# Differential heads: the low part of the keys beside zeros, so that every product of the scores works on 128 rows

## The chip, the cores and the metric

One core of a Trainium2 chip runs the whole program in one launch. The metric is device microseconds of that core, the median of several runs. The engines are named as the profile names them: PE is the tensor engine (PEld its weight loads), DVE the vector engine, ACT the scalar engine, POOL the gpsimd engine, SP the queue that starts the DMAs.

## What is computed

Two transformer blocks over 512 tokens of width 2048, all in float32. The first block has 16 meta tokens ahead (528 in all), eight grouped-query heads with an axial rope, and eight differential heads; the second has stick-breaking attention and a gated linear recurrence. The change is in the differential heads, each of which has two maps of 64 features:

```
q1, q2 = q[:, :, 0], q[:, :, 1]        # 64 features each
k1, k2 = k[:, :, 0], k[:, :, 1]
s1 = einsum('bhqd,bhkd->bhqk', q1, k1) * scale + bias
s2 = einsum('bhqd,bhkd->bhqk', q2, k2) * scale + bias
a  = softmax(s1) - lam * softmax(s2)
o  = einsum('bhqk,bhkd->bhqd', a, v)
```

## The kernel before

Precision comes from splits: a float32 operand becomes a high part, rounded to float32r, and a low part, the rest. A product is then three products: high with high, high with low and low with high. ACT rounds (line 148), DVE subtracts (line 149). The projections do this over 16 tiles of 128 rows (`fm` and `tm`, PSUM tile `pj`); their weights come from `in_wp` half a unit (512 KB) at a time, are split into the tile `wsp` (three buffers) and are consumed in a fixed sequence.

The order of PE is written out at tracing: projections (`main_work`) and all other pieces (`sides`) are generators, and `run` takes the next step of the first of them whose keys are there by a modelled clock. Each PE instruction is chained to the one before, so PE's order is fixed. The other engines take their instructions in the order that a scheduler gives them, each queue first in, first out.

The differential heads' scores are `b_scores` (lines 649 to 700), once per head h. With 64 features per map, the 128 rows of the array hold two things: plane m of the tile `qq` (`q2t`) has the high part of map m's queries in 64 of its rows and the low part in the other 64, and plane m of the tile `kk` (`kb`) has the high part of map m's keys in both halves. One product of 128 rows so gives high with high plus low with high. The third product, high with low, takes the 64 rows of `q2t` that hold the high part, and plane 2 of `kb`, where rows 0 to 63 hold the low part of map 0's keys and rows 64 to 127 that of map 1's.

`scores(qt, m, l)` does this for 128 queries (qt) and one map (m); the 528 keys go in two halves c of 264 columns into the PSUM tile `pss` (one buffer). So one call has four products on PE, two of 128 rows and then two of 64:

```
mm(s[:, c, :HL], q2t[:, m, qsl], kb[:, m, c * HL : (c + 1) * HL], True, False)          # line 674
mm(s[:, c, :HL], q2t[rows, m, qsl], kb[rows, 2, c * HL : (c + 1) * HL], False, True)    # line 676
```

There are 8 heads x 4 query tiles x 2 maps = 64 calls. DVE adds the distance bias and takes the row minimum out of `pss` (line 680), which frees it; ACT takes the exponential (683); DVE joins the two maps (693 to 696) into a tile `e`, which `pv_steps` transposes through `ptt` and `pmt` and multiplies with the values. The copies into `kb` are lines 660 to 663 (ACT) and 664, 665 (DVE); the bias table of a head is line 653 (POOL). Each head asks for a new tile `kk`, of which there is one buffer, so a head's copies wait until the head before has done with the whole tile. The grouped-query heads use the tile name too: line 559 takes 4 planes of 528 (high and low keys of two key heads), and `a_scores` has six products of 128 rows and 264 columns per query tile.

Of the kernel before, what the change touches and what calls it, by code (L numbers as in the profile page):

```python
# [74 lines left out]


def _sequence():
    """The order in which the weight units are used; the last column pairs of the first output projection and
    the first projections of the second block are read twice, for the two halves of the tokens."""
    seq = [("VA", 0), ("VA", 1)] + [("QA0", kg) for kg in range(4)]  # L80
    seq += [("GA", i) for i in range(8)] + [("QA1", kg) for kg in range(4)] + [("GB", i) for i in range(8)]
    for h in range(8):
        seq += [("QB", h), ("KB", h), ("VB", h)]
    seq += [("O1", 0, kg) for kg in range(3)] + [("O1", 1, kg) for kg in range(4)] + [("O1", 0, 3)]
    seq += [("O1", n, kg) for _ in range(2) for n in (2, 3) for kg in range(4)]
    seq += [("XL", b) for _ in range(2) for b in range(8)]
    seq += [("GL", b) for b in range(8)] + [("GS", b) for b in range(8)]
    for c in range(4):
        if c % 2 == 0:
            seq += [("v", c // 2, kg) for kg in range(4)]  # L90
        seq += [("qk", c, kg) for kg in (QK_LAST if c == 3 else range(4))]
    seq += [("O2", n, kg) for n in range(4) for kg in (0, 2, 3)] + [("O2", n, 1) for n in range(4)]
    return [(("KA", i), h) for h in range(2) for i in range(2)] + [(u, h) for u in seq for h in range(2)]
# [3 lines left out]
def hybrid_two_block_kernel(ctx: ExitStack, tc: tile.TileContext, wp, xT, xtok, par, lvec, cst, rg, pg, lruw, out):  # L97
# [9 lines left out]
    def T(shape, tag, dt=F32, bufs=1):  # L107
        return sb.tile(shape, dt, tag=tag, name=tag, bufs=bufs)
# [11 lines left out]
        return pss_pool[0].tile([P, 2, 512], F32, tag="pss", name="pss")  # L120

    def pst_banks():
        """The two banks as tiles of their own."""
        return pss_pool[0].tile([P, 512], F32, tag="bank", name="bank", bufs=2)

    def ptt():
# [33 lines left out]
            dve.scalar_tensor_tensor(y, t, 1.5, y, op0=ALU.add, op1=ALU.mult)  # L160
        return y

    # ------------------------------------------------- the tensor engine's order
    # The projections and the pieces of everything else are generators; the tensor engine takes their
    # instructions in the order traced here. A step waits for keys: `ready` has the time by which what a
    # key names is there, counted in the time of the products traced so far (`clock`).
    order_only = mybir.DependencyInfo(mybir.DependencyClass.NoSync, mybir.DependencyReason.DATA)
    state = {"clock": 0.0, "last": None}
    ready = {"pss": 0.0, "ptt": 0.0, "pmt": 0.0, "pt": 0.0, "calm": 0.0}
# [79 lines left out]
        o, n = PAR_COLS[name]  # L249
        return prm[:, o : o + n]  # L250

    # ------------------------------------------------- weights
    AHEAD = 2
    seq = _sequence()
    loaded = []

    def load_next(n=1024):
        """The next half unit, in pieces of n columns."""
        if len(loaded) == len(seq):
            return  # L260
        unit, h = seq[len(loaded)]
        raw = T([P, 1024], "wraw", F32, 3)
        w = T([P, 2, 1024], "wsp", F32R, 3)
        loaded.append(w)
        for c in range(0, 1024, n):
            nc.sync.dma_start(raw[:, c : c + n], wp[UIDX[unit], h, :, c : c + n])
            split(w[:, 0, c : c + n], w[:, 1, c : c + n], raw[:, c : c + n])
            if c + n < 1024:
                yield
# [12 lines left out]
    PASSES = ((0, 0), (0, 1), (1, 0))  # L282

    def fm(unit, ps, after_kt=None):
        """Features on partitions; ps: list of (PSUM AP, token columns of big)."""
        for kt in range(KT):
            if kt % 8 == 0:
                w = take(unit, kt // 8)
            for pi, (ws, xs) in enumerate(PASSES):
                lhs = w[:, ws, (kt % 8) * P : (kt % 8 + 1) * P]  # L290
                for ap, (a, b) in ps:
                    mm(ap, lhs, big[:, xs, kt, a:b], kt == 0 and pi == 0, kt == KT - 1 and pi == 2)
                yield
            if after_kt:
                after_kt(kt)

    def fm_two(units, ps, lag):
        """Two units side by side, the second one some steps behind."""
        w = [None, None]
        for i in range(KT + lag):  # L300
            for u, kt in ((0, i), (1, i - lag)):
                if 0 <= kt < KT:
                    if kt % 8 == 0:
                        w[u] = take(units[u], kt // 8)
                    for pi, (ws, xs) in enumerate(PASSES):
                        for c in range(2):
                            mm(ps[u][:, c, :HL], w[u][:, ws, (kt % 8) * P : (kt % 8 + 1) * P],
                               big[:, xs, kt, c * HL : (c + 1) * HL], kt == 0 and pi == 0, kt == KT - 1 and pi == 2)
                        yield
            if i == KT - 1:  # L310
                act.copy(halves(kvraw[0]), ps[0][:, :, :HL])
                post(("kv", 0), 1000)
# [5 lines left out]
        return fm(unit, [(ps[:, 0, :], (x0, x0 + NTOK))])  # L318

    def tm(units, x0, evac, kgs=range(4), toks=range(NT), before_unit=None, after_unit=None, chore=None):  # L320
        """Tokens on partitions; evac(token tiles, their sums) takes the results pair by pair;
        chore: a piece of work for every other step."""
        tiles = {p: pjt() for p in sorted({t // 2 for t in toks})}
        accs = {t: tiles[t // 2][:, t % 2, :] for t in toks}
        for i, unit in enumerate(units):
# [27 lines left out]
                after_unit(kg)  # L353
        post("calm", 2500)

    # ------------------------------------------------- constants, tokens
    act.preload_act_table_set("natural_log_exp_and_others")
    nc.sync.dma_start(prm, par)
    make_identity(nc, ident)
# [49 lines left out]
        dve.tensor_scalar(hg[:, 0:1], par_of("subg"), 0.5 * (1.0 - LAMBDA_INIT), None, op0=ALU.mult)  # L409
        dve.tensor_scalar(hg[:, 1:2], par_of("gq2"), P ** -0.5, None, op0=ALU.mult)  # L410

    # columns of ar in the first block
    kvraw = [ar[:, i * L : (i + 1) * L] for i in range(4)]
    CB = 2560
    cq, sq_ = ar[:, CB : CB + 512], ar[:, CB + 512 : CB + 1024]
# [5 lines left out]
    qs_, ks_, vs_ = ar[:, 4608:5120], ar[:, 5120:5648], ar[:, 2560:3088]  # L421
    osb, osq, orr = ar[:, 3088:3600], ar[:, 3600:4112], ar[:, 1824:2336]

    # ------------------------------------------------- shared pieces
    def diag(r, n=P):
        dg = et(P)
        dve.tensor_scalar(dg[:n, :n], ident[:n, :n], r, None, op0=ALU.mult)
# [14 lines left out]
        split(big[:, 0, s, :NTOK], big[:, 1, s, :NTOK], ybuf[:, s, :])  # L442

    def rope(x, rn, n, c, s, t1, u):
        """x [P, n, 128] (normalised in place), rn [P, n]; the result lands in t1."""
        v4 = lambda a: a.rearrange("p n (h two c) -> p n h two c", h=2, two=2)
        dve.tensor_tensor(x, x, rn.unsqueeze(2).broadcast_to([P, n, P]), ALU.mult)  # L447
        dve.tensor_tensor(blocks(t1), x, blocks(c), ALU.mult)
        for a in range(2):
            pool.tensor_tensor(v4(blocks(u))[:, :, :, a, :], v4(x)[:, :, :, 1 - a, :], v4(blocks(s))[:, :, :, a, :],  # L450
                               ALU.mult)
        dve.tensor_tensor(t1, t1, u, ALU.add)

    def tile_cols(j):
        """Columns of the real tokens' tiles, and of the meta tokens as the last one."""
        return slice(NM + j * P, NM + (j + 1) * P) if j < NT else slice(0, NM)

    def v_tiles(src, tail_i, r=None):
        """src [P d, L]: halves with tokens on partitions, the meta tokens stacked in vtail."""
        vt = T([P, 2, 4, P], "vv", F32R, 2)  # L460
        tp = flat(pst())
        for j in range(5):
# [15 lines left out]
        return vt, vs  # L478

    def pv_steps(h, tag, e, cols, vt, vs, use, extra=()):  # L480
        """Weighted sums over the keys, by halves of the queries; use(half, sums) takes them."""
        for hf in range(2):
            yield when("pt", "ptt", (tag, h, 2 * hf))
            hold("pt")
# [29 lines left out]
            post("pmt", 1300)  # L514
            use(hf, o)

    # ------------------------------------------------- side work, first block
    kt_ = [None]
    va = [None, None]
    lnload = [None, None]  # L520

    def side_norms():
        ready[("start", -1)] = 14000.0
# [125 lines left out]
    def b_scores(h, e):  # L649
# [6 lines left out]
        act.copy(q2t[64:128, 1], qs_[64:128])  # L656
        dve.tensor_tensor(q2t[64:128, 0], qs_[0:64], f(q2t[0:64, 0]), ALU.subtract)
        dve.tensor_tensor(q2t[0:64, 1], qs_[64:128], f(q2t[64:128, 1]), ALU.subtract)
        kb = T([P, 3, L], "kk", F32R)
        act.copy(kb[0:64, 0], ks_[0:64])  # L660
        act.copy(kb[64:128, 1], ks_[64:128])
        act.copy(kb[64:128, 0], ks_[0:64])
        act.copy(kb[0:64, 1], ks_[64:128])
        dve.tensor_tensor(kb[0:64, 2], ks_[0:64], f(kb[0:64, 0]), ALU.subtract)
        dve.tensor_tensor(kb[64:128, 2], ks_[64:128], f(kb[64:128, 1]), ALU.subtract)
        post(("qkused", h))
        post(("qkb", h), 6000)

        def scores(qt, m, l):
            rows = slice(64 * m, 64 * m + 64)  # L670
            qsl = slice(qt * P, (qt + 1) * P)
            s = pst()
            for c in range(2):
                mm(s[:, c, :HL], q2t[:, m, qsl], kb[:, m, c * HL : (c + 1) * HL], True, False)
            for c in range(2):
                mm(s[:, c, :HL], q2t[rows, m, qsl], kb[rows, 2, c * HL : (c + 1) * HL], False, True)
            x = et()
            nm = small(1)
            b0 = 384 - qt * P
# [49 lines left out]
        post(("normed", h))  # L729
        post(("y", 8 + h), 5000)  # L730

    # ------------------------------------------------- between the blocks
    yt = blocks(yflat, D)
    pgb = ar[:, 0:2048]

# [40 lines left out]
        if p:  # L776
            room["e"] = 4

    # ------------------------------------------------- RG-LRU
    cw = par_of("cw").rearrange("p (b i) -> p b i", i=4)  # L780
    cb = par_of("cb")

# [55 lines left out]
                dve.scalar_tensor_tensor(y, ybuf[:, i, :], 0.5, y, op0=ALU.mult, op1=ALU.mult)  # L838
                post(("xlused", i))

    # ------------------------------------------------- stick breaking
    raws = [blocks(ar[:, i * 2048 : (i + 1) * 2048], 512) for i in range(3)]
    gains = (hg[:, 1:2], par_of("gk2"))

# [78 lines left out]
        post(("sums", h))  # L923
        post(("ys", h), 1500)

    # ------------------------------------------------- projections
    def main_work():
        ps = [pjt(), pjt()]
        yield from fm_two((("KA", 0), ("KA", 1)), ps, 3)
# [230 lines left out]
    run(main_work(), sides)  # L1160


# [1 line left out]
def _pack(inputs):  # L1164
    import numpy as np

# [74 lines left out]
```

## Time and profile before

| what | value |
|---|---|
| median of 3 runs | 1752.49 us (1752.18 to 1752.86) |
| span of the profiled execution, first to last instruction | 1751.1 us |
| what lies around that span, against the median | 1.4 us |
| PE busy | 1739.6 us, 99% |
| DVE, ACT, POOL busy | 58%, 45%, 5% |
| mean granted TensorE clock | 1.000 (2.4 GHz) |
| differential heads' scores on PE | 431 to 823 us |

The page gives the span of the profiled execution, not its time as the runs count it; the runs' median is 1.4 us above the span. A PE "busy" of 99% says that PE is hardly ever without an instruction in flight; it does not say that it takes a new one as soon as it could, since matmuls overlap and their ends are modelled. The starts of successive instructions tell the latter.

### The profile page before, as it was taken

Reading aid. Unit: us, or ns where it says so; the run is one execution under the profiler, and the core shown is the slowest. Engines: PE = TensorE matmul, PEld = TensorE weight load, DVE = VectorE, ACT = ScalarE, POOL = GpSimd, SP = SyncE. Lnnn points to the kernel's source line nnn. Section 1 sums busy time; section 2 is a strip of 40 time slices with the busy share of each in tenths; the row PEclk is TensorE's granted clock in tenths of the full one; section 3 lists DMA queues with packets and bytes.
Section 4 is the critical chain, followed back from the end, with each engine's and each line's share of the span. In section 5 each row is a group of like instructions: output and inputs, shape, how many; then the busy total and the mean of one; then the engine's idle time right before and its main releaser. Section 6 shows DMA issues by size and latency. Waiting matters only on the chain.

```text
span 1751.1 us, 23788 instructions
## 1 busy us (share of the span) xinstructions
PE 1739.6 (99%) x9496; PEld 1484.8 (85%) x9496; DVE 1023.0 (58%) x1694; ACT 785.5 (45%) x1276; POOL 89.6 (5%) x83
## 2 busy tenths in 40 slices
PE   8999999999999999999999999999999999999998
PEld 8888888889998888988788998888888888888887
DVE  5748635863566666785458858843323564575433
ACT  6334423443445454564345537832222654564311
POOL 0101001100001100100000001100000000010000
PEclk9999999999999999999999999999999999999999
DMA  9321222212221222212367653222222222432223
GB/s 312 117 97 60 73 73 87 82 61 85 73 73 61 67 67 73 71 63 73 120 216 269 213 196 122 91 97 96 97 95 90 80 72 85 137 117 84 85 91 126
DMA packets 53854, 185.81 MB, mean 106 GB/s; under 512 B 6112, under 2 KB 7776, under 8 KB 52064
## 3 DMA queue, kind: packets, MB, share of 16 engines
q1 hardware_dynamic: 53744, 184.30, 31.7%
q8 instruction: 74, 1.21, 0.3%
q14 instruction: 36, 0.29, 0.1%
HBM read 175.89 MB, written 8.39 MB: 105 GB/s over the span
## 4 chain that ended last, share of the span: by engine, by line
PE 94%; DVE 2%; DMA 1%; issue 1%; ACT 0%; POOL 0%; SPq 0%; DVEq 0%; ACTq 0%; POOLq 0%
PE pj L181 81%; PE pss L181 4%; PE pmt L181 4%; PE ptt L184 2%; PE pmt L184 1%; PE bank L181 1%; PE pss L184 1%; DVE wsp L149 0%; DMA ybuf<-in_xtok 0%; DMA wraw<-in_wp 0%; DMA e<-in_xT 0%; ACT wsp L148 0%; POOL ar L450 0%; POOL ybuf L450 0%; DVE big L376 0%
## 5 line engine op out<-in xcount | busy, mean ns | idle before, releaser
L181 PE MATMUL pj<-big,wsp 128*128 128x264 f32 (+2 forms) x4608 | 814.9, 333 | 6.2 <-ACT big L375 5.4
L181 PEld LDWEIGHTS pj<-big,wsp 128*128 128x128 f32 x4608 | 687.8, 189 | 94.9 <-ACT big L375 5.4
L181 PE MATMUL pj<-wsp,big 128*128 128x512 f32 x3072 | 737.5, 397 | 0.6 <-DVE big L149 0.6
L181 PEld LDWEIGHTS pj<-wsp,big 128*128 128x128 f32 x3072 | 569.8, 188 | 132.3 <-DVE big L149 0.9
L149 DVE TENSOR_TENSOR wsp<-wraw,wsp 128x1024 fp32r<-128x1024 f32 (+1 forms) x299 | 363.3, 1215 | 389.1 <-ACT wsp L148 388.7
L148 ACT CAST wsp<-wraw 128x1024 fp32r<-128x1024 f32 (+1 forms) x299 | 310.8, 1040 | 504.9 <-PE pj L181 400.3
L683 ACT ACTIVATE e<-e,sm 128x528 f32<-128x528 f32 x64 | 47.2, 737 | 91.9 <-DVE sm L680 91.5
L148 ACT CAST pt<-ptt 128x512 fp32r<-128x512 f32 (+2 forms) x96 | 50.4, 525 | 77.5 <-PE ptt L184 77.3
L181 PE MATMUL pss<-kk,qq 128*128 128x264 f32 x448 | 83.6, 301 | 0.0
L149 DVE TENSOR_TENSOR pt<-ptt,pt 128x512 fp32r<-128x512 f32 (+2 forms) x96 | 59.5, 619 | 35.9 <-ACT pt L148 35.1
L181 PEld LDWEIGHTS pss<-kk,qq 128*128 128x128 f32 x448 | 66.8, 188 | 12.8 <-issue 0.2
L181 PEld LDWEIGHTS pmt<-pt,vv 128*128 128x128 f32 x528 | 69.1, 190 | 3.6
L680 DVE CUSTOM_DVE_ANT_0 e<-pss,ar 128x528 f32<-128x528 f32 x64 | 45.1, 704 | 45.8 <-PE pss L181 45.5
L181 PE MATMUL pmt<-pt,vv 128*128 128x256 f32 (+1 forms) x528 | 69.6, 280 | 0.0
L184 PE MATMUL ptt<-ident,e 128*128 128x128 f32 x336 | 52.6, 273 | 0.1
L184 PEld LDWEIGHTS ptt<-ident,e 128*128 128x128 f32 x336 | 40.6, 140 | 7.0 <-DVE e L626 0.5
L432 DVE TENSOR_TENSOR e<-pj,rbc 128x512 f32<-128x512 f32 x32 | 22.0, 688 | 39.8 <-PE pj L181 39.8
L881 POOL TENSOR_SCALAR_AFFINE_SELECT e<-e 128x128 f32<-128x128 f32 x32 | 15.7, 490 | 476.2 <-ACT e L880 474.2
L653 POOL TENSOR_SCALAR ar<-ar 128x912 f32<-128x912 f32 x8 | 22.5, 2816 | 262.5 <-DVE sm L680 257.9
L623 ACT ACTIVATE e<-pss,sm 128x528 f32<-128x528 f32 x32 | 22.4, 701 | 23.5 <-DVE sm L621 23.4
L450 POOL TENSOR_TENSOR ar<-ar 128x256 f32<-128x256 f32 x16 | 18.4, 1172 | 242.9 <-DVE ar L447 242.9
L890 ACT ACTIVATE e<-e 128x128 f32<-128x128 f32 (+3 forms) x32 | 15.0, 470 | 28.8 <-DVE e L889 28.5
(200 smaller groups left out, 1175.5 us busy)
## 6 DMA issues: line engine op xcount, KB each, us to landing
wraw<-in_wp SPq DMA_DIRECT2D x295, 512.0 KB, 3.5
e<-in_xT SPq DMA_DIRECT2D x16, 264.0 KB, 4.6
ybuf<-in_xtok SPq DMA_DIRECT2D x4, 1024.0 KB, 6.8
ar<-in_xtok SPq DMA_DIRECT2D x4, 1024.0 KB, 5.6
h1d<-ybuf SPq DMA_DIRECT2D x4, 1024.0 KB, 5.3
ybuf<-h1d SPq DMA_DIRECT2D x12, 256.0 KB, 3.5
out<-ybuf SPq DMA_DIRECT2D x12, 256.0 KB, 2.2
ar<-in_pg SPq DMA_DIRECT2D x1, 1024.0 KB, 4.8
```

The source lines that it names most:

```text
L148: act.copy(hi, src)
L149: dve.tensor_tensor(lo, src, f(hi), ALU.subtract)
L181: _queue(nc.tensor.matmul(out, lhsT, rhs, start=start, stop=stop).ins, cost)
L184: _queue(nc.tensor.transpose(out, in_, identity).ins, 110.0)
L432: dve.tensor_tensor(g, g_ps, rb, ALU.mult)
L450: pool.tensor_tensor(v4(blocks(u))[:, :, :, a, :], v4(x)[:, :, :, 1 - a, :], v4(blocks(s))[:, :, :, a, :], ALU.mult)
L623: act.activation(halves(x), sv, AF.Exp, bias=nm, accum_out=l[:, 0:1])
L653: pool.tensor_scalar(bias, dist, 2.0 ** (-(h + 1)), None, op0=ALU.mult)
L680: dve.tensor_tensor_reduce(out=halves(x), in0=s[:, :, :HL], in1=halves(bias[:, b0 : b0 + L]), scale=1.0, scalar=3e38, op0=ALU.add, op1=ALU ...
L683: act.activation(x, x, AF.Exp, scale=-1.0, bias=nm, accum_out=l[:, m : m + 1])
L881: pool.affine_select(z[:, t * P : w], z[:, t * P : w], [[-1, P]], ALU.is_gt, -1e30, base=0, channel_multiplier=1)
L890: act.activation(c, c, AF.Exp)
```

## The change

`kb` is now one tile of four planes, taken once, in head 0; planes 2 and 3 hold the low part of the keys of map 0 (rows 0 to 63) and of map 1 (rows 64 to 127), and the other 64 rows of each are set to zero once, by POOL. The third product then takes all 128 rows of `q2t[:, m]` and of plane 2 + m: the low part of the queries meets zeros. The rest of the diff removes comments and is left out.

```diff
+    kb_ = [None]
...
-        kb = T([P, 3, L], "kk", F32R)
+        if h == 0:
+            kb_[0] = T([P, 4, L], "kk", F32R)
+            pool.memset(f(kb_[0][64:128, 2]), 0.0)
+            pool.memset(f(kb_[0][0:64, 3]), 0.0)
+        kb = kb_[0]
         act.copy(kb[0:64, 0], ks_[0:64])
         act.copy(kb[64:128, 1], ks_[64:128])
         act.copy(kb[64:128, 0], ks_[0:64])
         act.copy(kb[0:64, 1], ks_[64:128])
         dve.tensor_tensor(kb[0:64, 2], ks_[0:64], f(kb[0:64, 0]), ALU.subtract)
-        dve.tensor_tensor(kb[64:128, 2], ks_[64:128], f(kb[64:128, 1]), ALU.subtract)
+        dve.tensor_tensor(kb[64:128, 3], ks_[64:128], f(kb[64:128, 1]), ALU.subtract)
...
         def scores(qt, m, l):
-            rows = slice(64 * m, 64 * m + 64)
             qsl = slice(qt * P, (qt + 1) * P)
             s = pst()
             for c in range(2):
                 mm(s[:, c, :HL], q2t[:, m, qsl], kb[:, m, c * HL : (c + 1) * HL], True, False)
             for c in range(2):
-                mm(s[:, c, :HL], q2t[rows, m, qsl], kb[rows, 2, c * HL : (c + 1) * HL], False, True)
+                mm(s[:, c, :HL], q2t[:, m, qsl], kb[:, 2 + m, c * HL : (c + 1) * HL], False, True)
```

The lines of the changed kernel lie 1 lower up to the copies into `kb` (653 becomes 654), 4 to 5 lower behind them (660 becomes 665, 664 and 665 become 669 and 670, 680 becomes 684, 683 becomes 687). PE's order of instructions is the same, and so are the numbers of instructions on PE, ACT, DVE and SP. Two things move.

ACT, between the scores of head 0 and head 1 (L683 is the exponential, 660 to 663 the copies into `kk`; `pt`, `ptail`, `ar` belong to the weighted sums of head 0). Before:

```order
L501 CAST ptail<-pmt 16x256
L683 ACTIVATE e,sm<-e,sm 128x528
L706 ACTIVATE ar<-pmt 128x256
L707 COPY ar<-pmt 128x256
L148 CAST wsp<-wraw 128x1024
L660 CAST kk<-ar 64x528
L661 CAST kk<-ar 64x528
L662 CAST kk<-ar 64x528
L683 ACTIVATE e,sm<-e,sm 128x528
L663 CAST kk<-ar 64x528
```

And in the changed kernel (687 is the exponential, 665 to 668 the copies):

```order
L501 CAST ptail<-pmt 16x256
L665 CAST kk<-ar 64x528
L667 CAST kk<-ar 64x528
L687 ACTIVATE e,sm<-e,sm 128x528
L710 ACTIVATE ar<-pmt 128x256
L711 COPY ar<-pmt 128x256
L148 CAST wsp<-wraw 128x1024
L666 CAST kk<-ar 64x528
L668 CAST kk<-ar 64x528
L687 ACTIVATE e,sm<-e,sm 128x528
```

The two copies into plane 0 now stand ahead of the exponential of the last query tile's map 0, and both copies into plane 1 ahead of that of map 1; the same happens, in one form or another, ahead of each of the heads 1 to 7. On DVE the subtraction into plane 2 moves ahead in the same places (line 680, an ISA row, is the one that frees `pss`). Before:

```order
L680 ISA e,sm<-pss,ar 128x528
L680 ISA sm 128x1
L149 TENSOR_TENSOR wsp<-wraw,wsp 128x1024
L680 ISA e,sm<-pss,ar 128x528
L680 ISA sm 128x1
L664 TENSOR_TENSOR kk<-ar,kk 64x528
L665 TENSOR_TENSOR kk<-ar,kk 64x528
```

And in the changed kernel:

```order
L684 ISA e,sm<-pss,ar 128x528
L684 ISA sm 128x1
L669 TENSOR_TENSOR kk<-ar,kk 64x528
L149 TENSOR_TENSOR wsp<-wraw,wsp 128x1024
L684 ISA e,sm<-pss,ar 128x528
L684 ISA sm 128x1
L670 TENSOR_TENSOR kk<-ar,kk 64x528
```

The subtraction 669 now stands ahead of the weights' split and of the 684 of the last map. POOL gets two fills behind the first bias table:

```order
L654 TENSOR_SCALAR ar<-ar 128x912
L662 MEMSET kk 64x528
L663 MEMSET kk 64x528
L654 TENSOR_SCALAR ar<-ar 128x912
L729 TENSOR_TENSOR ar<-ar 128x512
```

Before, the two bias tables of heads 0 and 1 followed each other there.

## Rows read from the trace of the kernel before

**Rows 1.** The page, parts 1 and 2: busy times, and tenths in 40 slices.

```profile
PE 1739.6 (99%) x9496; PEld 1484.8 (85%) x9496; DVE 1023.0 (58%) x1694; ACT 785.5 (45%) x1276; POOL 89.6 (5%) x83
...
PE   8999999999999999999999999999999999999998
...
PEclk9999999999999999999999999999999999999999
```

**Rows 2.** The page, part 4: the chain that ended last, by engine.

```profile
PE 94%; DVE 2%; DMA 1%; issue 1%; ACT 0%; POOL 0%; SPq 0%; DVEq 0%; ACTq 0%; POOLq 0%
```

**Rows 3.** Groups by line and shape: busy us, mean ns | idle before.

```profile
L181 PE MATMUL pss<-kk,qq 128*128 128x264 f32 x320 | 55.6, 288 | 0.0
L181 PEld LDWEIGHTS pss<-kk,qq 128*128 128x128 f32 x320 | 47.9, 189 | 3.7
L181 PE MATMUL pss<-kk,qq 64*128 64x264 f32 x128 | 32.5, 333 | 0.0
L181 PEld LDWEIGHTS pss<-kk,qq 64*128 64x128 f32 x128 | 18.9, 185 | 9.1 <-issue 0.2
```

**Rows 4.** Timeline of PE, head 0's first scores: start us, length us, instructions.

```profile
431.16 0.41 PE L181 MATMUL pss<-kk,qq 128*128 128x264 f32 x2
431.49 0.51 PE L181 MATMUL pss<-kk,qq 64*128 64x264 f32 x2
431.93 0.52 PE L181 MATMUL pj<-big,wsp 128*128 128x264 f32 x2
432.16 0.41 PE L181 MATMUL pj<-big,wsp 128*128 128x264 f32 x2
432.28 0.41 PE L181 MATMUL pj<-big,wsp 128*128 128x264 f32 x2
```

**Rows 5.** Timeline of PE, grouped-query scores: six products, then the next step.

```profile
351.46 0.89 PE L181 MATMUL pss<-kk,qq 128*128 128x264 f32 x6
352.19 0.62 PE L181 MATMUL pj<-big,wsp 128*128 128x512 f32 x2
...
389.11 0.89 PE L181 MATMUL pss<-kk,qq 128*128 128x264 f32 x6
389.83 1.55 PE L181 MATMUL pj<-big,wsp 128*128 128x512 f32 x6
```

**Rows 6.** Timeline of PE, a middle and the last call of scores.

```profile
474.80 0.85 PE L181 MATMUL pss<-kk,qq 128*128 128x264 f32 x4
475.58 1.24 PE L181 MATMUL pj<-big,wsp 128*128 128x264 f32 x8
...
482.59 0.84 PE L181 MATMUL pss<-kk,qq 128*128 128x264 f32 x4
...
822.10 0.84 PE L181 MATMUL pss<-kk,qq 128*128 128x264 f32 x4
822.88 1.20 PE L181 MATMUL pj<-wsp,big 128*128 128x512 f32 x4
```

**Rows 7.** Timeline of the weight loads at head 0's first scores.

```profile
431.04 0.31 PEld L181 LDWEIGHTS pss<-kk,qq 128*128 128x128 f32 x2
431.49 0.29 PEld L181 LDWEIGHTS pss<-kk,qq 64*128 64x128 f32 x2
431.93 0.19 PEld L181 LDWEIGHTS pj<-big,wsp 128*128 128x128 f32 x1
```

**Rows 8.** Timeline of PE: a product of 96 rows between products of 128.

```profile
526.15 0.28 PE L181 MATMUL pmt<-ptail,vtail 96*128 96x256 f32 x1
526.27 0.41 PE L181 MATMUL pj<-big,wsp 128*128 128x264 f32 x2
```

**Rows 9.** POOL: the first bias table (timeline), and a fill (groups by line).

```profile
350.04 2.50 POOL L653 TENSOR_SCALAR ar<-ar 128x912 f32<-128x912 f32 x1 [4.56 <-DVE e L626]
...
L360 POOL MEMSET ones<- 128x128 f32 x1 | 0.2, 204 | 0.0
```

**Rows 10.** Timeline of DVE, head 0's and head 1's keys; then of ACT.

```profile
427.05 0.70 DVE L665 TENSOR_TENSOR kk<-ar,kk 64x528 fp32r<-64x528 f32 x1
...
477.65 1.34 DVE L665 TENSOR_TENSOR kk<-ar,kk 64x528 fp32r<-64x528 f32 x1
...
478.52 0.63 ACT L663 CAST kk<-ar 64x528 fp32r<-64x528 f32 x1
```

**Rows 11.** Busy us in stretches of the heads (PE, PEld, DVE, ACT, POOL; clock, DMA share).

```profile
460.00:510.00 50.00, 50.00 (x348) 45.59 (x347) 31.44 (x58) 23.98 (x46) 4.61 (x2) 1.00 0.23 73
...
760.00:810.00 50.00, 50.00 (x255) 40.80 (x254) 36.72 (x69) 27.11 (x55) 4.30 (x2) 1.00 0.20 64
```

**Rows 12.** Timeline of DVE, then PE, where `pss` is freed latest.

```profile
761.21 0.08 DVE L680 DVE_READ_ACCUMULATOR2_ANT sm<- 128x1 f32 x1
761.21 2.49 DVE L149 TENSOR_TENSOR big<-ybuf,big 128x512 fp32r<-128x512 f32 x4
763.62 0.69 DVE L680 CUSTOM_DVE_ANT_0 e<-pss,ar 128x528 f32<-128x528 f32 x1
...
762.10 0.84 PE L181 MATMUL pss<-kk,qq 128*128 128x264 f32 x4
```

**Rows 13.** Who waited for whom: total us, times, longest us.

```profile
ACT wsp L148 <- PE pj L181: 400.3, 159, 8.7
```

## The prediction

> **What bounds the kernel now.** Read the page first: PE is busy for 99% of the span, in every slice but the first and the last 9 tenths or more, at a granted clock of 9 tenths or more throughout (the 2.4 GHz level) [rows 1], and 94% of the chain that ended last is PE [rows 2]. So PE sets the end, and time can only be won on PE. The page cannot say whether PE's instructions follow each other as closely as they could, for a matmul's end is modelled and its neighbours overlap. Groups by line with shapes apart give a first hint: the products of 64 rows and 264 columns take 333 ns on the mean, those of 128 rows and the same columns 288 [rows 3]. Half as many rows take longer, not less.
>
> The timeline of PE tells how much, by starts. The plain case first: a grouped-query score is six products of 128 rows and 264 columns, and the next step starts 0.73 and 0.72 us after the first of them (351.46 to 352.19, 389.11 to 389.83) [rows 5]: 0.121 us a product. Now one call of the differential scores [rows 4]: its first product starts at 431.16, the third projection product behind it at 432.28. That is 1.12 us for six steps (two products of 128 rows, two of 64, two of the projection), where six plain ones take 6 x 0.121 = 0.726. **0.394 us too much.** The starts show where it lies. Between the first product at 431.16 and the first of 64 rows at 431.49 there are two steps in 0.33 instead of 0.242. From there to the first projection product is 0.44 for two steps (0.242), and 0.23 for the next one (0.121), after which the pace is 0.12 again (432.16 to 432.28). The weight loads say the same: they run on without a gap except for 0.14 us ahead of the first load of 64 rows (431.35 to 431.49) and 0.15 us ahead of the first of 128 rows behind them (431.78 to 431.93) [rows 7]. So PE lets what is in flight come to its end twice per call: where it goes from 128 rows to 64, and where it comes back. A count of rows other than 128 is not enough for that: the product of 96 rows is followed after 0.12 us (526.15 to 526.27) [rows 8].
>
> It is the same from the first call to the last of 64: from the first product of a call to the first projection product there are 0.77 us in the first call [rows 4], 0.78 in the eighth and in the last (474.80 to 475.58, 822.10 to 822.88) [rows 6], for four steps that plainly take 0.484; the rest, 0.11, falls behind them as above.
>
> **The change part by part.**
>
> The third product on 128 rows: 128 matmuls keep their columns, and their weight load stays one of 128 columns (185 ns with 64 rows, 189 with 128 [rows 3]). The nearest row for the new form is the grouped-query score, the same tiles, the same shape, the same accumulation into two banks in turn: 0.121 us a product [rows 5]. So the two interruptions go and nothing takes their place: 64 calls x 0.394 us = **25.2 us**. How far can this be off? From below: if the engine's own durations were all there is, the gain would be 128 x (0.333 - 0.288) = 5.8 us [rows 3]. If only the idle time of the weight loads came back, it would be 64 x (0.14 + 0.15) = 18.6 us [rows 7]. From above: a rounding of 0.01 us per call, 0.6 us in all. I take 25.2, since starts count everything between two instructions whoever is charged with it, and keep 18.6 as a lower bound of the mechanism; the 5.8 is a lower bound only of what is booked.
>
> The Trainium skill, "TensorEngine Tiling (Array Packing)", section "Key Properties", says that a change of the tiling mode drains the tensor engine, and "TensorE: Matmul & The Clock Gate", section "Single matmul latency", puts a drain at some 175 ns. By these the 128 changes of mode would be an estimated 22.4 us, and the time 1730.1; the rows have 0.197 us per change, a little more, and I go by the rows.
>
> The zeros: two fills of 64 rows and 528 columns, on POOL, once. A fill of 128 columns took 0.204 us there [rows 9], so 0.2 to 0.85 us each. Behind the first bias table, which ended at 352.54 [rows 9], they wait for the last grouped-query scores, which start at 389.11 and are over by 390.0 [rows 5]; the first product that needs them starts at 431.49 [rows 4]. Some 40 us hide them, and nothing else stands on POOL before head 1's bias table. Cost: nothing; with the cover gone, 1.7 us at most.
>
> The copies into `kk`: since one tile serves all heads, a copy waits for the last reader of its own plane and no longer for the whole tile, so ACT and DVE take up to half of them before the last map of the head before. No copy is added. They leave earlier, which shortens the way to the next head's first scores; that way had some 3.6 us to spare already (subtraction done at 478.99 [rows 10], scores at 482.59 [rows 6]). The price is that the exponential of map 0 waits for two more ACT copies (0.63 us each [rows 10]), and its tile `e` is late by that much at most. Cost: nothing on PE, by that spare time.
>
> What is late next: PE runs 0.4 us faster per call, so every other queue has 3.2 us less per head. The weights don't suffer: ACT's splits wait 400.3 us in total for PE to free a buffer [rows 13], so PE paces them, and they come earlier with it. DVE is busy for 31.4 to 36.7 of 50 us [rows 11]; with 3.2 us less that is at most 36.7 of 46.8, 78%. The tightest place that I found is in head 6, where DVE frees `pss` at 761.29 and the next call starts at 762.10 [rows 12]: 0.8 us to spare, which the gain of two calls (2 x 0.394) would use up if DVE did not move at all. PE may touch DVE there, for a few tenths.
>
> **The sum.** 1751.1 - 25.2 = 1725.9 us of span, and with the 1.4 us that lie between this span and the median, **1727.3 us**, 1.4% less.
>
> **The rivals.**
>
> *The rows are not the cause.* The gaps could come from something else that the third product does, its wait on DVE's subtraction or its place in the accumulation, and stay: 1752.5. For it: the change leaves PE's order as it is, and a product's time need not depend on its rows. Against it: the gap behind the second product of 64 rows precedes a projection product that waits for nothing, the gap is the same in every call, and six products accumulate in the same manner without one [rows 5]. The Trainium skill speaks for this rival in "TensorE: Matmul & The Clock Gate", section "Why this matters for your kernels": a single matmul of 32 rows takes the same time as one of 128, the gain of few rows being concurrency. Inside the pair of 64 rows the trace agrees as far as the durations go; at its two edges it does not, 0.33, 0.44 and 0.23 us where equal steps would have 0.24, 0.24 and 0.12.
>
> *Part is given back to DVE.* In the last two heads DVE also splits the output projection's features and frees `pss` late [rows 12]. If PE there gained nothing, because each call waited for DVE, 16 calls x 0.394 = 6.3 us would be lost: 1733.6. For it: 0.8 us of slack, and 36.7 of 50 us busy. Against it: DVE is idle for 13 of the 50 us [rows 11], so it catches up between such pieces.
>
> *Slower: DVE and ACT become the bound.* The subtraction into `kk` now stands on DVE ahead of the instruction that frees `pss` for the last map, and behind ACT's copies; copies that wait for PE hold up the weights' splits and the exponentials behind them in ACT's queue. To end slower by more than can be told, each of the 64 calls would have to wait 0.394 + 0.055 us beyond its present slack, say 1.3 us with the 0.8 of the tightest place. A subtraction of 0.70 to 1.34 us [rows 10] reaches that only if it always fell into the slack, and it moves in seven places, not 64. At the full 1.34 us in each of these and no slack at all it costs 9.4 us, still short of 25.2. It would need a stall of 4 us per head; then 1756 or more.
>
> **How the numbers follow.** A measurement of this kernel can tell about 0.2%, 3.5 us, from no change. The forecast, 0.83: 1727.3, by itself 1724.5 to 1729 (1.4 us for what lies around the span, 0.7 for the spread of the runs, 0.6 for rounding below it; a few tenths of DVE above). Part given back, 0.09: up to 1733.6. Rows not the cause, 0.06: 1752.5, in a sixth of it 1746.7, the 5.8 of the durations. Slower, 0.02. The range takes in the forecast and what is given back: 1724.5 to 1733.6; the bound by the weight loads, 1733.9, is its upper end too. Faster: 0.83 + 0.09 + 0.01 = 0.93. Same: 0.05. Slower: 0.02.
>
> **What would show it.** Right: no product of 64 rows is left; from a call's first product to the next projection product are 0.48 to 0.50 us; the group of `pss<-kk,qq` has 448 products at 285 to 290 ns; the scores end near 798 instead of 823, and all stages behind them have their old lengths. POOL has two new fills before 400 us. Part given back: PE has idle time before `pss` products, released by DVE's line 684, late in the heads. Wrong: the steps of a call keep 0.77 us with 128 rows, or the stage of the heads is as long as before, with waits on DVE or ACT where there are none now.

## The result and the profile after

| | before | changed |
|---|---|---|
| median of 4 runs each | 1752.67 us (1752.18 to 1753.2) | 1728.35 us (1727.61 to 1728.67) |
| span of the profiled execution | 1751.1 us | 1725.8 us |
| PE busy | 1739.6 us | 1714.7 us |

The changed kernel is faster: 24.3 us, a ratio of 0.9858 (95% interval 0.9846 to 0.9870). The forecast was 1727.3 in a range of 1724.5 to 1733.6.

The page's parts 1 and 4 after the change, beside [rows 1, 2]:

```profile
PE 1714.7 (99%) x9496; PEld 1477.6 (86%) x9496; DVE 1015.9 (59%) x1694; ACT 783.8 (45%) x1276; POOL 91.0 (5%) x85
...
PE 96%; DVE 2%; issue 0%; DMA 0%; POOL 0%; ACT 0%; SPq 0%; DVEq 0%; ACTq 0%; POOLq 0%
```

PE's share is 99% as before, over a span 25.3 us shorter: the share could not have shown that there was anything to win. What answers to [rows 3], groups by line and shape:

```profile
L181 PE MATMUL pss<-kk,qq 128*128 128x264 f32 x448 | 71.4, 287 | 0.0
L181 PEld LDWEIGHTS pss<-kk,qq 128*128 128x128 f32 x448 | 63.5, 188 | 3.7
```

The products of 64 rows are gone, and the 9.1 us of idle weight loads ahead of them too. Their booked time fell by 16.7 us (55.6 + 32.5 before, 71.4 after), less than what was won. The projection products beside them were booked with less time as well: 4.5 us for those of 264 columns (256.8 before, 252.3 after), 2.4 us for those of 512. The timeline of PE at the first and the last call, which answers to [rows 4, 6]:

```profile
430.45 0.65 PE L181 MATMUL pss<-kk,qq 128*128 128x264 f32 x4
430.94 1.86 PE L181 MATMUL pj<-big,wsp 128*128 128x264 f32 x14
...
797.23 0.65 PE L181 MATMUL pss<-kk,qq 128*128 128x264 f32 x4
797.72 1.09 PE L181 MATMUL pj<-wsp,big 128*128 128x512 f32 x4
```

A call goes over to the next projection product after 0.49 us where it took 0.77 and 0.78, and the pace of 0.12 us is kept behind it. From the first call to the product behind the last one there were 391.72 us (431.16 to 822.88); now there are 367.27 (430.45 to 797.72). So 24.45 of the 25.3 us of span lie in this stage, and most of the rest is the 0.71 us by which this execution came to it earlier, which differs from run to run (430.5 to 432.1 us in the profiles of this study).

### The profile page after: what moved, and what is told of

Same layout as the page of the kernel before. It is cut to its first block, busy times and chain, and to the rows that moved or that the text cites. A ratio compares the mean times of both kernels' runs of the same rounds, so it can differ in the third digit from the quotient of the medians.

```text
span 1725.8 us, 23791 instructions
## 1 busy us (share of the span) xinstructions
PE 1714.7 (99%) x9496; PEld 1477.6 (86%) x9496; DVE 1015.9 (59%) x1694; ACT 783.8 (45%) x1276; POOL 91.0 (5%) x85
## 4 chain that ended last, share of the span: by engine, by line
PE 96%; DVE 2%; issue 0%; DMA 0%; POOL 0%; ACT 0%; SPq 0%; DVEq 0%; ACTq 0%; POOLq 0%
PE pj L181 84%; PE pmt L181 4%; PE pss L181 4%; PE ptt L184 2%; PE pmt L184 1%; PE bank L181 1%; PE pss L184 1%; DVE wsp L149 0%; DMA wraw<-in_wp 0%; POOL ybuf L450 0%; SPq L374 0%; ACT wsp L148 0%; POOL ar L450 0%; SPq L266 0%; DVE sm L574 0%
## 5 line engine op out<-in xcount | busy, mean ns | idle before, releaser
L181 PE MATMUL pss<-kk,qq 128*128 128x264 f32 x448 | 71.4, 287 | 0.0
L624 ACT ACTIVATE e<-pss,sm 128x528 f32<-128x528 f32 x32 | 22.4, 701 | 23.5 <-DVE sm L622 23.4
```

The lines of the kernel that those rows point to most:

```text
L181: _queue(nc.tensor.matmul(out, lhsT, rhs, start=start, stop=stop).ins, cost)
L624: act.activation(halves(x), sv, AF.Exp, bias=nm, accum_out=l[:, 0:1])
```

## The experiments

The theory: PE is held up where it goes from products of 128 rows to products of 64 and where it comes back, by some 0.197 us each time, and nothing else in the change matters. Each ratio is against runs of the kernel before that were taken beside it; their medians are 1752.72 us for the first four runs below, 1753.04 for the next four and 1752.73 for the last.

**Rows alone.** The old tile of three planes, taken once per head, with products of 128 rows:

```diff
-            rows = slice(64 * m, 64 * m + 64)
...
-                mm(s[:, c, :HL], q2t[rows, m, qsl], kb[rows, 2, c * HL : (c + 1) * HL], False, True)
+                mm(s[:, c, :HL], q2t[:, m, qsl], kb[:, 2, c * HL : (c + 1) * HL], False, True)
```

Expected:

> The kernel before with one edit: the third product takes all 128 rows of the old plane 2, where the other 64 rows hold the low part of the other map's keys in place of zeros, so the scores get a term that does not belong there (this leaves out the zeros). Tile per head, copies and fills as before. Theory (each change between products of 128 and of 64 rows costs PE 0.197 us, two per call): 1727 to 1729, as the changed kernel. Rival (the gain comes from the tile that serves all heads, whose copies leave earlier): no gain, 1752 to 1754. Rival (both share): in between, near 1740.

Measured: 1728.22 us (ratio 0.9859, 0.9842 to 0.9875). The whole gain is there without the single tile, the fills or the earlier copies, and without zeros: what stands in the other rows plays no part in the time.

**The tile alone.** The changed kernel with the third product on 64 rows:

```diff
+            rows = slice(64 * m, 64 * m + 64)
...
-                mm(s[:, c, :HL], q2t[:, m, qsl], kb[:, 2 + m, c * HL : (c + 1) * HL], False, True)
+                mm(s[:, c, :HL], q2t[rows, m, qsl], kb[rows, 2 + m, c * HL : (c + 1) * HL], False, True)
```

Expected:

> The changed kernel with the third product back on 64 rows (rows 64m to 64m+63 of planes 2 and 3); one tile for all heads, fills and earlier copies stay. Theory: the two changes per call are back, 64 x 0.394 = 25.2 us, so 1752 to 1754. Rival (the tile and the earlier copies make the gain): 1727 to 1730. If the fills or the earlier copies cost something that the gain hid, this is slower than the kernel before, above 1754.

Measured: 1753.26 us, ratio 1.0002 (0.9992 to 1.0011). So the tile, the fills and the reordered copies give nothing and cost nothing that can be told.

**Twice as many changes.** The kernel before with the products of a call in the order high, low, high, low:

```diff
             for c in range(2):
                 mm(s[:, c, :HL], q2t[:, m, qsl], kb[:, m, c * HL : (c + 1) * HL], True, False)
-            for c in range(2):
                 mm(s[:, c, :HL], q2t[rows, m, qsl], kb[rows, 2, c * HL : (c + 1) * HL], False, True)
```

Expected:

> The kernel before with the four products of a call in another order: high of half 0, low of half 0, high of half 1, low of half 1. So 128 and 64 rows alternate, four changes per call in place of two, with the same products, waits and copies. Theory: another 64 x 0.394 = 25.2 us, 1776 to 1780. Rival (the gap belongs to the first wait on the low part or to the return to the projections): once per call as before, 1752 to 1755. Rival (a third product directly behind a product of its own bank costs something by itself): the order control with 128 rows alone is then slower as well.

Measured: 1777.4 us, ratio 1.0140 (1.0125 to 1.0155), 24.7 us more than before. The timeline of PE at the first call, narrow stretches:

```profile
430.77 0.28 PE L181 MATMUL pss<-kk,qq 128*128 128x264 f32 x1
430.99 0.39 PE L181 MATMUL pss<-kk,qq 64*128 64x264 f32 x1
431.30 0.39 PE L181 MATMUL pss<-kk,qq 128*128 128x264 f32 x1
431.62 0.38 PE L181 MATMUL pss<-kk,qq 64*128 64x264 f32 x1
431.93 0.39 PE L181 MATMUL pj<-big,wsp 128*128 128x264 f32 x1
```

The products of 64 rows start at 430.99 and 431.62, and the projection product at 431.93: a call takes 1.16 us to it in place of 0.77. No wait of the original is doubled here, nor any product; only the changes are, and the price doubles. In these traces the product behind a change has its start where its own weight load starts (431.49 in [rows 4] and in [rows 7]), other products some 0.12 us behind theirs (431.16 and 431.04). So a step from one kind of start to the other is not to be read alone. The three steps between the last four rows are of one kind: 0.31 to 0.32 us, 0.19 to 0.20 more than the plain 0.12.

**The same order on 128 rows**, its control: the changed kernel with the second `for c` taken out in the same way. Expected:

> The changed kernel with the order of the run with four changes, all on 128 rows: the control for the order. Theory: nothing changes, 1727 to 1730. Rival (consecutive products into one bank wait for each other): above 1735.

Measured: 1728.67 us (ratio 0.9862, 0.9847 to 0.9876), as the changed kernel. Two products in a row into one bank cost nothing here, so the order is not what made the run with four changes slow.

**Half of the calls.** The changed kernel with map 1 back on 64 rows:

```diff
+            rows = slice(64 * m, 64 * m + 64) if m else slice(0, P)
             for c in range(2):
-                mm(s[:, c, :HL], q2t[:, m, qsl], kb[:, 2 + m, c * HL : (c + 1) * HL], False, True)
+                mm(s[:, c, :HL], q2t[rows, m, qsl], kb[rows, 2 + m, c * HL : (c + 1) * HL], False, True)
```

Expected:

> The changed kernel with the third product of map 1 back on 64 rows (rows 64 to 127 of plane 3), map 0 on 128 rows; nothing is left out. Theory: half of the changes are back, 32 x 0.394 = 12.6 us, 1740 to 1742. Rival (the time follows from a wait for DVE or ACT that only sets in past some number of calls): either 1728 or 1752.

Measured: 1740.22 us (ratio 0.9928, 0.9913 to 0.9943), 11.9 us above the changed kernel. So 0, 64, 128 and 256 changes stand at 1728.35, 1740.22, 1753.26 and 1777.4 us: 0.19 us a change on the whole, (1777.4 - 1728.35) / 256. The traces say it more sharply. From the first call to the product behind the last one there are 367.27 us in the changed kernel, 379.50 here (431.72 to 811.22), 391.72 before and 416.56 with 256 changes (430.77 to 847.33): 0.191, 0.191 and 0.193 us a change, counted from none.

**Other counts of rows.** 96 rows for map 0, in the changed kernel:

```diff
+            n = 96 if m == 0 else P
             for c in range(2):
-                mm(s[:, c, :HL], q2t[:, m, qsl], kb[:, 2 + m, c * HL : (c + 1) * HL], False, True)
+                mm(s[:, c, :HL], q2t[:n, m, qsl], kb[:n, 2 + m, c * HL : (c + 1) * HL], False, True)
```

Expected:

> The changed kernel with 96 rows in place of 128 in the third product of map 0 (rows 0 to 95: the low part and 32 rows of zeros, so nothing is left out), map 1 as changed. In the trace of the kernel before a product of 96 rows is followed after 0.12 us. Theory (96 rows are no change): 1727 to 1730. Rival (any count other than 128 costs): 32 x 0.394 = 12.6 us more, 1740 to 1742.

And 32 rows in the kernel before:

```diff
-            rows = slice(64 * m, 64 * m + 64)
+            rows = slice(64 * m, 64 * m + 32)
```

Expected:

> The kernel before with 32 rows in place of 64 in the third product (rows 64m to 64m+31: half of the features' low part is left out). If each change to a smaller count of rows costs the same whatever the count: 1752 to 1754. If the price grows with how few rows are used: above 1755. If it is half at 32 rows: 1740.

Measured: 1727.73 us with 96 rows (ratio 0.9857, 0.9842 to 0.9872), 1752.99 with 32 (1.0000, 0.9990 to 1.0010). Groups by line and shape, first the run with 96 rows:

```profile
L181 PE MATMUL pss<-kk,qq 96*128 96x264 f32 x64 | 13.0, 285 | 0.0
L181 PEld LDWEIGHTS pss<-kk,qq 96*128 96x128 f32 x64 | 10.0, 189 | 0.0
```

and the run with 32:

```profile
L181 PE MATMUL pss<-kk,qq 32*128 32x264 f32 x128 | 32.3, 331 | 0.0
L181 PEld LDWEIGHTS pss<-kk,qq 32*128 32x128 f32 x128 | 18.7, 183 | 9.1 <-issue 0.2
```

96 rows are like 128: 285 ns, no idle weight load. 32 rows are like 64: 331 ns against 333, and the same 9.1 us of idle loads ahead of them. So the price is for crossing from 128 rows to 64 or 32 and back, and 32 cost no more than 64. Between 64 and 96 rows nothing was tried, nor other numbers of columns.

**The other rows.** The kernel before, where the second of the two products of 64 rows takes the other half of the rows:

```diff
+                o = rows if c == 0 else slice(64 - 64 * m, 128 - 64 * m)
-                mm(s[:, c, :HL], q2t[rows, m, qsl], kb[rows, 2, c * HL : (c + 1) * HL], False, True)
+                mm(s[:, c, :HL], q2t[o, m, qsl], kb[o, 2, c * HL : (c + 1) * HL], False, True)
```

Expected:

> The kernel before, where the second of a call's two products of 64 rows takes the other 64 rows (so half of the scores get the other map's product in place of their own low part; that part is left out). Both products stay at 64 rows. If the price is for the change between 128 and 64 rows alone: 1752 to 1754, as before. If every change of the rows in use costs 0.197 us: one more per call, 12.6 us, 1765. If products of 64 rows on different rows run beside each other: up to 0.1 us per call less, 1745 to 1752.

Measured: 1745.28 us (ratio 0.9956, 0.9942 to 0.9971), 7.8 us less than before, 0.12 us per call: one product's step. PE's timeline, and the timeline of the weight loads, in a stretch of 0.01 us at the first call:

```profile
432.43 0.39 PE L181 MATMUL pss<-kk,qq 64*128 64x264 f32 x2
...
432.43 0.19 PEld L181 LDWEIGHTS pss<-kk,qq 64*128 64x128 f32 x2
```

Both loads lie in one stretch of 0.19 us and both products in one of 0.39: they run side by side. The Trainium skill, "TensorE: Matmul & The Clock Gate", section "Why this matters for your kernels", says so of products of few rows on different row groups; the trace agrees. With two changes per call this form still is 17 us behind the 128 rows. Going from one half of the rows to the other is no third change.

**How much room the side engines leave.** The changed kernel without the third product (high queries with low keys are left out), PE's order otherwise kept:

```diff
-                mm(s[:, c, :HL], q2t[:, m, qsl], kb[:, m, c * HL : (c + 1) * HL], True, False)
-            for c in range(2):
-                mm(s[:, c, :HL], q2t[:, m, qsl], kb[:, 2 + m, c * HL : (c + 1) * HL], False, True)
+                mm(s[:, c, :HL], q2t[:, m, qsl], kb[:, m, c * HL : (c + 1) * HL], True, True)
+            state["clock"] += 220.0
```

Expected:

> The changed kernel without the third product (the high part of the queries with the low part of the keys is left out of the scores); the modelled clock is advanced by its 220 ns, so PE's order stays the same but for the missing products. It asks how far PE can run ahead in the heads before DVE or ACT holds it up. Theory (PE alone sets the end, the side engines follow): 128 products fewer at 0.121 us, 15.5 us, so 1712 to 1714 and no idle time on PE at the scores. Rival (the room is used up: in the changed kernel the tightest call follows DVE's freeing of its tile at once): PE waits for DVE's line that frees the tile in the last two heads, up to 16 x 0.242 = 3.9 us are given back, 1714 to 1717, with that idle time in the trace.

Measured: 1713.44 us, 14.9 us below the changed kernel for 128 products fewer, 0.117 us each. Who waited for whom, PE's row in the stretch of the heads (total us, times, longest us):

```profile
PE pss L181 <- DVE sm L683: 0.4, 1, 0.4
```

L683 is here the line that frees `pss`, 684 in the changed kernel. One call waited 0.4 us for DVE, no other did. So even another 0.242 us per call would nearly all have reached the end.

## Why the prediction was right

*The sum.* 64 calls x 0.394 us = 25.2 us was forecast; the medians moved by 24.3, the stage by 24.45. The mechanism is the one that was named, two interruptions per call, shown by the row counts, by doubling and halving the changes and by doing each part of the change alone. The term came out 3% too large. It was read off one call, 0.394 us; the mean over the 64 calls of the two traces is 0.387 (0.772 us to the next projection product before against 0.490 after, and 0.105 us less in the step behind it). That is 0.5 of the 0.75 us; 0.1 us lies behind the last call, outside the stretch that was timed, and the rest was not traced further. Of the three ways to price it, the booked durations (5.8) and the idle weight loads (18.6) were both too small; the starts were right.

*The first hint.* That products of 64 rows take longer, 333 ns against 288 in [rows 3], was a sign of the interruption and not a slower product. Of the two in [rows 4] the first is booked from its weight load on, 0.39 us, and the second takes 0.28, as one of 128 rows does:

```profile
431.72 0.28 PE L181 MATMUL pss<-kk,qq 64*128 64x264 f32 x1
```

For the same reason the steps 0.33, 0.44 and 0.23 us do not tell how the 0.394 is shared between the edges; the equal steps of the run with four changes do.

*What lies around the span.* 1.4 us were added, and by the same reckoning it is 2.5 here. Both set a median beside the span of one execution. Each run that is listed with its own span took 1.7 to 1.9 us more than it, the profiled run of the changed kernel too (1727.61 against 1725.8), so nothing changed there. The sum did not suffer: 1751.1 + 1.4 is the median before, from which the 25.2 go off.

*The zeros.* Two fills, hidden. The timeline of POOL:

```profile
389.41 0.54 POOL L662 MEMSET kk<- 64x528 f32 x1 [37.59 <-PE pss L181]
390.00 0.53 POOL L663 MEMSET kk<- 64x528 f32 x1
```

They wait for the last grouped-query scores as forecast, take 0.54 us each, inside the bounds of 0.2 to 0.85, and are done 40 us before the first call needs them.

*The copies that leave earlier.* Forecast as free; the run with the tile alone shows it at the old pace of PE, at a ratio of 1.0002, and the run with rows alone at the new one: there the copies stay late, and it ends with the changed kernel (1728.22 and 1728.35).

*What is late next.* The call in head 6 was named as the place where PE might touch DVE. The timeline after the change, which answers to [rows 12] (DVE, then the weight loads of PE, then PE):

```profile
740.85 0.07 DVE L684 DVE_READ_ACCUMULATOR2_ANT sm<- 128x1 f32 x1
...
740.98 0.54 PEld L181 LDWEIGHTS pss<-kk,qq 128*128 128x128 f32 x4
...
740.99 0.74 PE L181 MATMUL pss<-kk,qq 128*128 128x264 f32 x4
741.57 0.64 PE L181 MATMUL pj<-big,wsp 128*128 128x264 f32 x4
```

The 0.8 us to spare have shrunk to 0.07 (740.92 to 740.99). DVE did not move: from the end of its last wait for PE to this release there are 12.82 us before (748.47 to 761.29) and now (728.10 to 740.92). PE came up to it, as argued, and just touches it. In the run without the third product, where the profile shows the same call waiting, PE also starts 0.06 us behind the release. And this call goes over to the next projection product after 0.58 us (740.99 to 741.57), all others after 0.48 to 0.50. So the touch costs some 0.09 us, where a few tenths were forecast. The rival that had the last two heads give back 6.3 us falls with it.

*The rival that the rows are not the cause* falls with the first run, and the order control takes its last form away. *Slower* needed 4 us of stall per head; the profile lists no wait of PE in the heads, and the starts show the 0.09 us above alone.

*By the Trainium skill* ("TensorE: Matmul & The Clock Gate", section "Single matmul latency") a drain of some 175 ns made an estimated 22.4 us; the runs have 0.19 us a change, 24.3 to 24.5, so the figure, which the page gives for a single bf16 product with its issue, is a little low here. By the Trainium skill ("TensorEngine Tiling (Array Packing)", section "Key Properties") a change of the tiling mode drains the engine; a pause of 0.19 us at every change agrees with that. That PE lets what is in flight come to its end, as the prediction also said, no trace here shows, since the ends of products are modelled: shown are the pauses, their number and their price.

## What to carry to other kernels

Where PE is busy all the time, read the starts of successive instructions and compare each group's step with the plain one of the same columns: here a call that took longer than its products was held up at the edges of the short ones. A crossing from 128 rows to 64 and back cost 0.38 us, with 32 rows the same, and a product of 64 rows with 64 rows of padding cost nothing more than one of 128. So fill up the rows, unless enough short products stand together on different halves behind one crossing. One such pair won back 0.12 of the 0.38 us; by these numbers it would take four pairs to gain, an estimate that no run here tested.

When PE gets faster, look for the place where another engine already frees its buffer late: it is touched first. It does not bound the rest. With 0.07 us left in that call, leaving out the third product still won 14.9 us, and the call itself gave 0.4 of it back.

## What the runs showed that was not expected

What 32 rows would cost was left open between three outcomes; they cost just what 64 do, 1752.99 us against 1753.04, while 96 cost nothing, 1727.73, as the theory had it. Two products of 64 rows on different halves, with weight loads of their own, were thought to win 0.1 us per call at the most. They ran fully side by side within an otherwise serial stream, which made a kernel that pays the same two crossings 7.8 us faster, 0.12 us per call.
